# Expert weights of a 16-expert block moved in runs of 22,528 bytes per partition

## The chip, the cores and the metric

The kernel runs on one core of a Trainium2 chip. The metric is device time in microseconds (us) of one execution. The core has a matrix engine (PE, with PEld for its weight loads), a vector engine (DVE), a scalar engine (ACT), GpSimd (POOL) and a sync engine (SP) that here only issues DMAs; 16 DMA engines carry those transfers. SBUF has 128 partitions.

## The reference

One encoder block on 512 tokens of width 1,024, all in float32: a mixer (four pooling windows and eight heads of differential attention, merged by gates) and then a mixture of 16 experts, in which each expert picks its 64 tokens of highest affinity. The change is in the second half:

```python
    logits = jnp.einsum('bsd,de->bse', h, w_router, preferred_element_type=jnp.float32)
    aff = jax.nn.softmax(logits, axis=-1)
    vals, idx = lax.top_k(aff.transpose(0, 2, 1), cap)
    xs = jax.vmap(lambda hb, ib: hb[ib])(h, idx.reshape(B, -1)).reshape(B, N_EXPERTS, cap, D)
    g = jnp.einsum('becd,edf->becf', xs, w_gate)
    u = jnp.einsum('becd,edf->becf', xs, w_up)
    y = jnp.einsum('becf,efd->becd', jax.nn.silu(g) * u, w_down) * vals[..., None].astype(h.dtype)
    flat = (jnp.arange(B)[:, None, None] * S + idx).reshape(-1)
    out = jax.ops.segment_sum(y.reshape(-1, D), flat, num_segments=B * S)
```

Each expert has three matrices of 1,024 x 2,816 (or 2,816 x 1,024) float32 numbers, so 11,534,336 bytes each and 34.6 MB for the three. The result is added to the block's stream and goes through a last RMS norm.

## The kernel before

The first half (to about 480 us of the profiled execution) computes the mixer. Its weights come through four small tiles `wraw` of 2 KB per partition (L130, in `load_next`), are split into a high and a low part by ACT and POOL into three tiles `whl`, and feed three-pass matmuls. The last of these matrices is `w_out`, eight pieces `k` of two loads each; its loop `out_proj` runs until about 530 us and reads eight tiles `m0` to `m7`.

The second half walks through the experts `e`. The token matrix `xs` of 64 tokens is the stationary operand, the weights are the moving one, and two column groups of PE work at a time (L726 and L727 in `colpair`, one for each half of the output rows). For one expert, in order:

- gate and then up: eight slices `k` of 2,816 columns each (L737), a slice being one `slot`, 128 partitions of 11,264 bytes. A slice takes six matmuls in three pairs.
- SiLU, product, and eleven transposes into `hT2`.
- down: 22 row blocks `f` of 1,024 columns, two to a slot (L762). In SBUF a slot's partition gets two runs of 4,096 bytes.
- the sum into `acc` through `vv` (L774, L776), while the routing of the next expert is computed by DVE in between.

`slot()` deals out 13 buffers in a ring: NS1 = 7 of pool `s1`, then NS2 = 6 of pool `s2`. `s1` lies where the tiles of the first half were and is free when they are; `s2` lies over `m0` to `m7`, `whl` and `wraw` and is free as `out_proj` gets through them. All weights are requested by SP, in program order. Each request waits until the last matmul on the slot's former contents is done, and also until the transfer eight requests earlier has landed, since eight semaphores (DMAHW0 to DMAHW7) are dealt out in turn to SP's transfers.

For the last expert the down matrix is taken in two column halves `n` (L784), each in six slots of up to two row blocks of either half `h`, and a slot in two transfers with runs of 2,048 bytes (L795). After `n` = 0 its sum and squares are done (L805), `acc` is put into the result banks of `n` = 1 (L788), and after `n` = 1 the norm and the output follow (L810 to L821).

The Bass context is made with the standard scratch for descriptors of DMAs that GpSimd issues (L891); it takes 16,384 bytes of each partition. GpSimd issues 32 such DMAs, all in the mixer (L382, L388).

Of the kernel before, what the change touches and what calls it, by code (L numbers as in the profile page):

```python
# [9 lines left out]
F32 = mybir.dt.float32  # L10
# [7 lines left out]
P = 128  # L18
S = 512
D = 1024  # L20
KT = D // P
# [3 lines left out]
F = 2816  # L25
FH = F // 2
NF = F // P
NFH = NF // 2
NE = 16
CAP = 64  # L30
# [4 lines left out]
CHUNKS = ((0, 512), (512, 512), (1024, 384))  # L35
# [26 lines left out]
 'pool': (2, 2, 2, 1, 1, 0, 0, 0),  # L62
 'fills': (1, 0.3, 2, 0.5, 2.5, 1.5, 2, 1, 0.5),
 'tabs': 1}
NS1, NS2 = 7, 6


def block_kernel(tc, a, out):
    nc = tc.nc
    V, A, G, T, SP = nc.vector, nc.scalar, nc.gpsimd, nc.tensor, nc.sync  # L70
# [5 lines left out]
    def cols(i, n=P):  # L76
        return slice(i * n, (i + 1) * n)
# [135 lines left out]
    with pool("st", side="right") as st:  # L213
        first = []
# [34 lines left out]
        for k in range(KT):  # L249
            for j in range(2):  # L250
                w = loaded[j]
# [242 lines left out]
    for h in range(NH):  # L494
# [13 lines left out]
        o = at.tile([P, S], F32, name="o", bufs=2)  # L508
# [33 lines left out]
    for d in range(KT):  # L542
        w = weights()
        ps = bank("ip")
# [27 lines left out]
    s1 = ctx.enter_context(pool("s1"))  # L572
# [72 lines left out]
    for k in range(KT - 2):  # L645
        w = weights()
# [19 lines left out]
    s2 = ctx.enter_context(pool("s2", side="right"))  # L666
# [51 lines left out]
    def slot():  # L718
        i = nslot[0] % (NS1 + NS2)
        nslot[0] += 1  # L720
        if i < NS1:
            return s1.tile([P, F], F32, name="sl1", bufs=NS1)
        return s2.tile([P, F], F32, name="sl2", bufs=NS2)

    def colpair(ps, n, lhsT, r0, r1, first, last):
        T.matmul(ps[0:CAP, :n], lhsT, r0, start=first, stop=last)  # L726
        T.matmul(ps[CAP:, :n], lhsT, r1, start=first, stop=last)  # L727

    cur = route(0, rk0)
    for e in range(NE):  # L730
        xs, ga = cur
        proj = []
        for wname in ("w_gate", "w_up"):
            ps = [gu() for _ in CHUNKS]
            for k in range(KT):
                w = slot()
                SP.dma_start(w, a[wname][e, k])  # L737
                for i, (c0, n) in enumerate(CHUNKS):
                    colpair(ps[i], n, xs[:, k], w[:, c0:c0 + n], w[:, FH + c0:FH + c0 + n],
                            k == 0, k == KT - 1)  # L740
            proj.append(ps)
            if wname == "w_gate":
                rk = rank(e + 1) if e + 1 < NE else None
                vv = route_v(ga)
        cur = route(e + 1, rk) if e + 1 < NE else None
        act = act_tile()
        for i, (c0, n) in enumerate(CHUNKS):
            A.activation(act[:, c0:c0 + n], proj[0][i][:, :n], AF.Silu)
            V.tensor_tensor(act[:, c0:c0 + n], act[:, c0:c0 + n], proj[1][i][:, :n], op=ALU.mult)  # L749
        hT2 = tr_tile()  # L750
        for j0 in range(0, NFH, 4):
            n = min(4, NFH - j0)
            pt = mx()
            for j in range(n):
                T.transpose(pt[:, cols(j)], act[:, cols(j0 + j)], ident)  # L755
            A.copy(hT2[:, j0:j0 + n], pt[:, :n * P].rearrange("p (j q) -> p j q", j=n))  # L756
        if e == NE - 1:
            break
        pd = mx()
        for f0 in range(0, NF, 2):  # L760
            w = slot()
            SP.dma_start(w[:, :2 * D].rearrange("p (f c) -> p f c", f=2), a["w_down"][e, f0:f0 + 2].rearrange("f p c -> p f c"))  # L762
            for j in range(2):
                f = f0 + j
                half, ft = divmod(f, NFH)
                colpair(pd, S, hT2[:, ft, cols(half, CAP)],
                        w[:, j * D:j * D + S], w[:, j * D + S:(j + 1) * D], f == 0, f == NF - 1)
        y = mw.tile([P, S], F32, name="y", bufs=2)
        A.copy(y, pd)
        for t in range(NTT):  # L770
            for n in range(2):
                pc = mx()
                r = cols(n, CAP)
                T.matmul(pc, vv[r, cols(t)], y[r], start=True, stop=True)  # L774
                c = cols(n, S)
                V.tensor_tensor(acc[:, t, c], (x1 if e == 0 else acc)[:, t, c], pc, op=ALU.add)  # L776
# [7 lines left out]
    for n in range(2):  # L784
# [2 lines left out]
            for t in range(NTT):  # L787
                T.matmul(fin[t], ident, acc[:, t, c], start=True, stop=False)  # L788
        pd = mx()
        for j0 in range(0, NFH, 2):  # L790
            nj = min(2, NFH - j0)
            w = slot()[:, :2 * nj * S].rearrange("p (h j c) -> p h j c", h=2, j=nj)
            for h in range(2):
                f0 = h * NFH + j0
                SP.dma_start(w[:, h], a["w_down"][NE - 1, f0:f0 + nj, :, c].rearrange("f p c -> p f c"))  # L795
            for j in range(nj):
                for h in range(2):
                    T.matmul(pd[cols(h, CAP)], hT2[:, j0 + j, cols(h, CAP)], w[:, h, j],  # L798
                             start=(j0 + j == 0), stop=(j0 + j == NFH - 1))
# [45 lines left out]
    return {"consts": cv, "border": border, "tie": tie, "slots": slots}  # L845


def _layout(i):
    x = i["x"].reshape(S, D)
    w_in = i["w_in"].reshape(D, -1)  # L850
# [5 lines left out]
    def pk(v):  # L856
# [18 lines left out]
        "w_out": i["w_out"].reshape(KT, P, D),  # L875
        "g_ffn": pk(i["g_ffn"]),
        "w_router": i["w_router"].reshape(KT, P, NE).transpose(1, 0, 2),
        "w_gate": i["w_gate"].reshape(NE, KT, P, F),
        "w_up": i["w_up"].reshape(NE, KT, P, F),
        "w_down": i["w_down"].reshape(NE, NF, P, D),  # L880
        "g_final": i["g_final"].reshape(1, D),
    }

# [18 lines left out]
```

## Time and profile before

| | us |
|---|---|
| median of 3 runs (1854.99 to 1856.50) | 1855.67 |
| profiled execution, span from the first to the last instruction | 1854.6 |
| PE busy | 1692.7 (91%) |
| DVE busy | 565.4 (30%) |
| ACT busy | 333.1 (18%) |
| POOL busy | 228.9 (12%) |
| all 19,979 instructions; transfers on SP's queue | 602.04 MB, 114,976 packets |

The page cuts the span into 40 slices of 46.4 us and prints for each the busy tenths of every engine, the clock granted to PE, the busy tenths of the DMA engines and the bytes moved. A group of instructions is then shown with its line, engine and tiles. The chain of waits goes back from the last instruction to what released it, step by step. Windows give busy times and bytes moved for any stretch.

### The profile page before, as it was taken

What the parts mean: (1) busy time and instruction counts of PE and PEld (TensorE: products, weight loads), DVE (VectorE), ACT (ScalarE), POOL (GpSimd) and SP (SyncE); (2) the same over time, 40 slices, a digit from 0 to 9 for tenths busy, and PEclk for the clock granted to TensorE, in tenths of its full rate; (3) what the DMA queues carried; (4) which work ended last, traced back from release to release, by engine and by line L of the source; (5) the groups of instructions that cost most, each with busy time, mean ns of one, the idle gap of its engine ahead of it and who ended that gap; (6) DMA issues with size and microseconds to landing.
All of it is one profiled execution on the core that took longest, in us unless ns stands there. A gap on an engine that the chain in (4) does not pass through costs nothing.

```text
span 1854.6 us, 19979 instructions
## 1 busy us (share of the span) xinstructions
PE 1692.7 (91%) x7980; PEld 826.2 (45%) x7980; DVE 565.4 (30%) x1313; ACT 333.1 (18%) x647; POOL 228.9 (12%) x193
## 2 busy tenths in 40 slices
PE   7999999999989999999898989889898988889887
PEld 5777888778853333333232323223232323323222
DVE  6965566753150212202021211202121220202102
ACT  4454545563221000000000000000000000000001
POOL 2543444545500000000000000000000000000000
PEclk9999999999999999999999999999999999999999
DMA  5332222222789999999999999999999999999996
GB/s 197 97 97 86 82 89 80 69 78 82 267 331 413 421 418 417 421 414 425 414 423 415 420 418 417 422 414 424 415 422 417 418 421 415 423 415 423 415 409 260
DMA packets 117629, 607.52 MB, mean 328 GB/s; under 512 B 11936, under 2 KB 12576, under 8 KB 84768
## 3 DMA queue, kind: packets, MB, share of 16 engines
q1 hardware_dynamic: 114976, 602.04, 80.5%
q0 software_dynamic: 2560, 4.20, 1.1%
q8 instruction: 63, 1.03, 0.2%
q14 instruction: 30, 0.25, 0.0%
HBM read 599.90 MB, written 2.10 MB: 325 GB/s over the span
## 4 chain that ended last, share of the span: by engine, by line
PE 46%; DMA 43%; DVE 6%; issue 2%; ACT 1%; POOL 1%; SPq 0%; DVEq 0%; ACTq 0%; POOLq 0%
DMA sl<-in_w_up_dram 15%; DMA sl<-in_w_gate_dram 14%; DMA sl<-in_w_down_dram 14%; PE gu L726 12%; PE mx L726 6%; PE ip L98 5%; PE ip L100 5%; PE ip L99 5%; PE mx L774 2%; PE mx L692 2%; PE sc L98 1%; PE sc L100 1%; PE sc L99 1%; PE mx L798 1%; PE sc L441 1%
## 5 line engine op out<-in xcount | busy, mean ns | idle before, releaser
L726 PE MATMUL gu<-sl,xs 128*64 128x512 f32 (+1 forms) x1536 | 631.5, 562 | 24.5 <-DMA sl<-in_w_up_dram 24.1
L727 PE MATMUL gu<-sl,xs 128*64 128x512 f32 (+1 forms) x1536 | 631.8, 562 | 0.0
L726 PEld LDWEIGHTS gu<-sl,xs 128*64 128x64 f32 x1536 | 203.6, 137 | 412.9 <-issue 363.5
L726 PE MATMUL mx<-sl,hT 128*64 128x512 f32 x660 | 305.8, 600 | 55.4 <-DMA sl<-in_w_down_dram 50.4
L727 PE MATMUL mx<-sl,hT 128*64 128x512 f32 x660 | 306.1, 600 | 0.0
L726 PEld LDWEIGHTS mx<-sl,hT 128*64 128x64 f32 x660 | 81.5, 136 | 266.2 <-issue 139.5
L727 PEld LDWEIGHTS gu<-sl,xs 128*64 128x64 f32 x1536 | 200.1, 137 | 0.0
L93 POOL TENSOR_TENSOR whl<-wraw,whl 128x512 fp32r<-128x512 f32 x122 | 174.4, 1449 | 191.5 <-ACT whl L91 191.2
L776 DVE TENSOR_TENSOR acc<-acc,mx 128x512 f32<-128x512 f32 x112 | 72.5, 685 | 409.6 <-PE mx L774 409.6
L814 POOL TENSOR_TENSOR fs<-fs,cv 128x1 f32<-128x1 f32 x4 | 2.2, 554 | 1314.2 <-DVE fs L812 1314.2
L749 DVE TENSOR_TENSOR act<-act,gu 128x512 f32<-128x512 f32 (+1 forms) x48 | 30.5, 640 | 425.1 <-PE gu L727 425.1
L774 PE MATMUL mx<-y,vv 64*128 64x512 f32 x240 | 100.5, 684 | 27.7 <-DVE acc L776 16.5
L91 ACT ACTIVATE whl<-wraw 128x512 fp32r<-128x512 f32 (+1 forms) x149 | 86.8, 621 | 102.8 <-PE ip L100 44.2
L98 PE MATMUL ip<-hT,whl 128*128 128x512 f32 x240 | 98.4, 410 | 0.0
L99 PE MATMUL ip<-hT,whl 128*128 128x512 f32 x240 | 95.3, 397 | 0.0
L100 PE MATMUL ip<-hT,whl 128*128 128x512 f32 x240 | 94.8, 395 | 0.0
L692 PE MATMUL mx<-x,gm 128*64 128x512 f32 x256 | 74.4, 616 | 17.1 <-DVE gm L687 17.1
L694 ACT COPY y<-mx 128x512 f32<-128x512 f32 x16 | 9.4, 586 | 431.5 <-PE mx L692 431.5
L601 DVE TENSOR_SCALAR_CACHE_REDUCE cmp<-mx,aff 128x384 f32<-128x384 f32 (+3 forms) x105 | 54.7, 521 | 104.8 <-PE mx L672 102.7
L756 ACT COPY hT<-mx 128x512 f32<-128x512 f32 (+1 forms) x48 | 24.9, 552 | 323.8 <-PE mx L755 323.7
L727 PEld LDWEIGHTS mx<-sl,hT 128*64 128x64 f32 x660 | 81.5, 136 | 0.0
L774 PEld LDWEIGHTS mx<-y,vv 64*128 64x128 f32 x240 | 32.8, 193 | 93.9 <-DVE acc L776 69.6
(219 smaller groups left out, 1965.7 us busy)
## 6 DMA issues: line engine op xcount, KB each, us to landing
sl<-in_w_gate_dram SPq DMA_DIRECT2D x128, 1408.0 KB, 23.7
sl<-in_w_up_dram SPq DMA_DIRECT2D x128, 1408.0 KB, 27.1
sl<-in_w_down_dram SPq DMA_DIRECT2D x165, 1024.0 KB, 18.9
wraw<-in_w_c_dram SPq DMA_DIRECT2D x79, 256.0 KB, 2.9
sl<-in_w_down_dram SPq DMA_DIRECT2D x20, 512.0 KB, 10.7
wraw<-in_w_v_dram SPq DMA_DIRECT2D x16, 256.0 KB, 2.9
wraw<-in_w_pool_out_dram SPq DMA_DIRECT2D x16, 256.0 KB, 2.8
wraw<-in_w_attn_out_dram SPq DMA_DIRECT2D x16, 256.0 KB, 2.9
```

The lines of the kernel that those rows point to most:

```text
L91: A.activation(dst_h, src, AF.Copy, scale=scale)
L93: (eng or V).tensor_tensor(dst_l, src, dst_h.bitcast(F32), op=ALU.subtract)
L98: T.matmul(ps, lh, rh, start=first, stop=False)
L99: T.matmul(ps, lh, rl, start=False, stop=False)
L100: T.matmul(ps, ll, rh, start=False, stop=last)
L601: V.tensor_scalar(scratch(src.shape[-1]), src, thr, None, op0=op, op1=ALU.add, accum_out=dst)
L692: T.matmul(px[cols(n, CAP)], gm[:, t], x1[:, t, cols(n, S)], start=(t == 0), stop=(t == NTT - 1))
L726: T.matmul(ps[0:CAP, :n], lhsT, r0, start=first, stop=last)
L727: T.matmul(ps[CAP:, :n], lhsT, r1, start=first, stop=last)
L749: V.tensor_tensor(act[:, c0:c0 + n], act[:, c0:c0 + n], proj[1][i][:, :n], op=ALU.mult)
L774: T.matmul(pc, vv[r, cols(t)], y[r], start=True, stop=True)
L776: V.tensor_tensor(acc[:, t, c], (x1 if e == 0 else acc)[:, t, c], pc, op=ALU.add)
```

## The change

Gate and up are stored in DRAM so that two slices `k` of a partition lie side by side; a transfer fills one slot of 22,528 bytes per partition, and the loop over `k` becomes one over pairs `k2`. The down matrix of experts 0 to 14 is stored as four blocks per expert, each 22,528 bytes per partition: 5.5 row blocks. Row blocks 5 and 16 are cut between two slots, each side with 256 of the 512 columns of either column group, so that these two take four narrower matmuls where two stood. The last expert's down matrix becomes an array of its own, `w_last`, laid out by column half; each half comes in pieces of 4, 4 and 3 and of 4, 3, 2, 1 and 1 row-block pairs, a piece being one transfer with one run per partition. The ring has seven slots of double size, four in `s1` and three in `s2`. The scratch for GpSimd's descriptors is 2,048 bytes.

```diff
-NS1, NS2 = 7, 6
+NS1, NS2 = 4, 3
+F2 = 2 * F
+DOWN = 4
+LAST = (((0, 4), (4, 4), (8, 3)), ((0, 4), (4, 3), (7, 2), (9, 1), (10, 1)))
+def down_rows(b):
+    lo, hi = 11 * b, 11 * (b + 1)
+    out = []
+    while lo < hi:
+        if lo % 2 or hi - lo == 1:
+            out.append((lo // 2, lo % 2))
+            lo += 1
+        else:
+            out.append((lo // 2, None))
+            lo += 2
+    return out
...
-            return s1.tile([P, F], F32, name="sl1", bufs=NS1)
-        return s2.tile([P, F], F32, name="sl2", bufs=NS2)
+            return s1.tile([P, F2], F32, name="sl1", bufs=NS1)
+        return s2.tile([P, F2], F32, name="sl2", bufs=NS2)
...
-            for k in range(KT):
-                w = slot()
-                SP.dma_start(w, a[wname][e, k])
-                for i, (c0, n) in enumerate(CHUNKS):
-                    colpair(ps[i], n, xs[:, k], w[:, c0:c0 + n], w[:, FH + c0:FH + c0 + n],
-                            k == 0, k == KT - 1)
+            for k2 in range(KT // 2):
+                wd = slot()
+                SP.dma_start(wd, a[wname][e, k2])
+                for j in range(2):
+                    k, w = 2 * k2 + j, wd[:, j * F:(j + 1) * F]
+                    for i, (c0, n) in enumerate(CHUNKS):
+                        colpair(ps[i], n, xs[:, k], w[:, c0:c0 + n], w[:, FH + c0:FH + c0 + n],
+                                k == 0, k == KT - 1)
...
-        for f0 in range(0, NF, 2):
+        for b in range(DOWN):
             w = slot()
-            SP.dma_start(w[:, :2 * D].rearrange("p (f c) -> p f c", f=2), a["w_down"][e, f0:f0 + 2].rearrange("f p c -> p f c"))
-            for j in range(2):
-                f = f0 + j
+            SP.dma_start(w, a["w_down"][e, b])
+            o = 0
+            for f, q in down_rows(b):
                 half, ft = divmod(f, NFH)
-                colpair(pd, S, hT2[:, ft, cols(half, CAP)],
-                        w[:, j * D:j * D + S], w[:, j * D + S:(j + 1) * D], f == 0, f == NF - 1)
+                r = slice(0, S) if q is None else cols(q, 256)
+                n = r.stop - r.start
+                lhsT = hT2[:, ft, cols(half, CAP)]
+                first, last = f == 0, f == NF - 1
+                T.matmul(pd[0:CAP, r], lhsT, w[:, o:o + n], start=first, stop=last)
+                T.matmul(pd[CAP:, r], lhsT, w[:, o + n:o + 2 * n], start=first, stop=last)
+                o += 2 * n
...
-        for j0 in range(0, NFH, 2):
-            nj = min(2, NFH - j0)
-            w = slot()[:, :2 * nj * S].rearrange("p (h j c) -> p h j c", h=2, j=nj)
-            for h in range(2):
-                f0 = h * NFH + j0
-                SP.dma_start(w[:, h], a["w_down"][NE - 1, f0:f0 + nj, :, c].rearrange("f p c -> p f c"))
+        for j0, nj in LAST[n]:
+            w = slot()[:, :2 * nj * S]
+            SP.dma_start(w, a["w_last"][n, :, 2 * j0 * S:2 * (j0 + nj) * S])
+            w = w.rearrange("p (j h c) -> p h j c", h=2, j=nj)
...
-        "w_gate": i["w_gate"].reshape(NE, KT, P, F),
+        "w_gate": i["w_gate"].reshape(NE, KT // 2, 2, P, F).transpose(0, 1, 3, 2, 4).reshape(NE, KT // 2, P, F2),
...
-    nc = _bacc.Bacc("TRN2", target_bir_lowering=False, num_devices=1)
+    nc = _bacc.Bacc("TRN2", target_bir_lowering=False, num_devices=1, dynamic_dma_scratch_size=2048)
```

On SP's queue at the start of the experts, the first weights are requested between the last loads of `w_out`. `sl1` and `sl2` are slots of the two pools; the names in brackets are the semaphores waited for. Before:

```order
L737 DMA sl1_4770<-in_w_gate_dram 128x2816 [waits DMAHW7_49,DVE_49]
L130 DMA wraw_4447<-in_w_out_dram 128x512 [waits DMAHW0_49,Pool_49]
L130 DMA wraw_4451<-in_w_out_dram 128x512 [waits DMAHW4_49,DMAHW1_49,Pool_49]
L737 DMA sl1_4778<-in_w_gate_dram 128x2816 [waits DMAHW2_49,DMASW1_49,DMASW0_49]
L130 DMA wraw_4480<-in_w_out_dram 128x512 [waits DMAHW5_49,DMAHW3_49,Pool_49]
L130 DMA wraw_4484<-in_w_out_dram 128x512 [waits DMAHW6_49,Pool_49]
L737 DMA sl1_4786<-in_w_gate_dram 128x2816 [waits PE_49]
L737 DMA sl1_4794<-in_w_gate_dram 128x2816 [waits PE_49]
L737 DMA sl1_4802<-in_w_gate_dram 128x2816 [waits DMAHW7_49]
L737 DMA sl1_4810<-in_w_gate_dram 128x2816 [waits DMAHW0_49]
L737 DMA sl1_4818<-in_w_gate_dram 128x2816 [waits DMAHW1_49]
L737 DMA sl2_4826<-in_w_gate_dram 128x2816 [waits DMAHW2_49,DVE_49,PE_49]
```

The same place of SP's queue now:

```order
L756 DMA sl1_4770<-in_w_gate_dram 128x5632 [waits DMAHW7_49,DVE_49]
L149 DMA wraw_4447<-in_w_out_dram 128x512 [waits DMAHW0_49,Pool_49]
L149 DMA wraw_4451<-in_w_out_dram 128x512 [waits DMAHW4_49,DMAHW1_49,Pool_49]
L149 DMA wraw_4480<-in_w_out_dram 128x512 [waits DMAHW5_49,DMAHW2_49,Pool_49]
L149 DMA wraw_4484<-in_w_out_dram 128x512 [waits DMAHW6_49,DMAHW3_49,Pool_49]
L756 DMA sl1_4784<-in_w_gate_dram 128x5632
L756 DMA sl1_4798<-in_w_gate_dram 128x5632 [waits PE_49]
L756 DMA sl1_4812<-in_w_gate_dram 128x5632
L756 DMA sl2_4854<-in_w_up_dram 128x5632 [waits DMAHW7_49,DVE_49,PE_49]
L756 DMA sl2_4868<-in_w_up_dram 128x5632 [waits DMAHW1_49,DMAHW2_49,DMAHW0_49,DMAHW3_49,PE_49,Pool_49]
L756 DMA sl2_4882<-in_w_up_dram 128x5632 [waits PE_49]
L756 DMA sl1_4896<-in_w_up_dram 128x5632 [waits PE_49]
```

The first transfer of weights is twice as large and stands ahead of all four last loads of `w_out`; then four slots of `s1` hold all of the first gate matrix, `s2` takes the first three pairs of slices of up (the first of these waits for the matmuls on `m4`, before it was `m2` for a single slice), and the fourth waits for the first two slices of gate to be used up.

On SP's queue at the end, the first column half of the last expert's down matrix (and after the change both halves). Before:

```order
L795 DMA sl1_9563<-in_w_down_dram 128x2x512 [waits DMAHW2_49,PE_49]
L795 DMA sl1_9563<-in_w_down_dram 128x2x512 [waits DMAHW3_49]
L795 DMA sl1_9570<-in_w_down_dram 128x2x512 [waits DMAHW4_49,PE_49]
L795 DMA sl1_9570<-in_w_down_dram 128x2x512 [waits DMAHW5_49]
L795 DMA sl2_9577<-in_w_down_dram 128x2x512 [waits DMAHW6_49,PE_49]
L795 DMA sl2_9577<-in_w_down_dram 128x2x512 [waits DMAHW7_49]
L795 DMA sl2_9584<-in_w_down_dram 128x2x512 [waits DMAHW0_49,PE_49]
L795 DMA sl2_9584<-in_w_down_dram 128x2x512 [waits DMAHW1_49]
L795 DMA sl2_9591<-in_w_down_dram 128x2x512 [waits DMAHW2_49,PE_49]
L795 DMA sl2_9591<-in_w_down_dram 128x2x512 [waits DMAHW3_49]
L795 DMA sl2_9598<-in_w_down_dram 128x512 [waits DMAHW4_49,PE_49]
L795 DMA sl2_9598<-in_w_down_dram 128x512 [waits DMAHW5_49]
```

Now, with the three pieces of the first half and the five of the second:

```order
L818 DMA sl2_9157<-in_w_last_dram 128x4096 [waits DMAHW1_49,PE_49]
L818 DMA sl1_9167<-in_w_last_dram 128x4096 [waits DMAHW2_49,PE_49]
L818 DMA sl1_9177<-in_w_last_dram 128x3072 [waits DMAHW3_49,PE_49]
L818 DMA sl1_9212<-in_w_last_dram 128x4096 [waits DMAHW4_49,PE_49]
L818 DMA sl1_9222<-in_w_last_dram 128x3072 [waits DMAHW5_49,PE_49]
L818 DMA sl2_9230<-in_w_last_dram 128x2048 [waits DMAHW6_49,PE_49]
L818 DMA sl2_9236<-in_w_last_dram 128x1024 [waits DMAHW7_49,PE_49]
L818 DMA sl2_9240<-in_w_last_dram 128x1024 [waits DMAHW1_49,DMAHW0_49,PE_49]
```

Twelve transfers of the first half become three; the last of them holds three row-block pairs, where the last of before held one.

## Rows read from the trace of the kernel before

**Rows 1.** The page's 40 slices: PE and DMA busy tenths, bytes moved.

```profile
PE   7999999999989999999898989889898988889887
...
DMA  5332222222789999999999999999999999999996
GB/s 197 97 97 86 82 89 80 69 78 82 267 331 413 421 418 417 421 414 425 414 423 415 420 418 417 422 414 424 415 422 417 418 421 415 423 415 423 415 409 260
```

**Rows 2.** The chain that ended last, shares of the span by line.

```profile
DMA sl<-in_w_up_dram 15%; DMA sl<-in_w_gate_dram 14%; DMA sl<-in_w_down_dram 14%; PE gu L726 12%; PE mx L726 6%; PE ip L98 5%; PE ip L100 5%; PE ip L99 5%; PE mx L774 2%; PE mx L692 2%; PE sc L98 1%; PE sc L100 1%; PE sc L99 1%; PE mx L798 1%; PE sc L441 1%
```

**Rows 3.** The chain in order of time: start, us, what; a DMA from issue to landing.

```profile
611.06 1.18 PE mx L774 x4
...
685.46 1.18 PE mx L774 x4
...
1004.38 27.10 DMA sl<-in_w_gate_dram
1031.54 28.26 DMA sl<-in_w_up_dram
...
1069.12 18.82 DMA sl<-in_w_down_dram
...
1668.87 27.11 DMA sl<-in_w_gate_dram
```

**Rows 4.** Waits of SP's queue: waited for, us in total, times, longest.

```profile
SPq L737 <- DMA sl<-in_w_gate_dram: 330.3, 112, 3.4
SPq L762 <- PE gu L727: 196.8, 77, 6.2
```

**Rows 5.** The page's packets, by size.

```profile
DMA packets 117629, 607.52 MB, mean 328 GB/s; under 512 B 11936, under 2 KB 12576, under 8 KB 84768
```

**Rows 6.** Windows: stretch, its us, busy us by engine, clock, DMA share, GB/s.

```profile
1008.00:1056.00 48.00, 44.65 (x210) 16.43 (x208) 12.93 (x41) 2.27 (x4) 0.00 (x0) 1.00 1.01 423
1060.00:1084.00 24.00, 20.17 (x93) 6.40 (x93) 2.50 (x5) 1.55 (x3) 0.00 (x0) 1.00 1.02 409
...
1144.00:1168.00 24.00, 20.17 (x93) 6.29 (x89) 2.50 (x5) 1.55 (x3) 0.00 (x0) 1.00 1.03 412
...
1812.00:1832.00 20.00, 18.55 (x58) 6.34 (x54) 5.09 (x8) 3.48 (x9) 0.00 (x0) 1.00 1.04 385
```

**Rows 7.** SP's requests at the experts' start, in order of time.

```profile
510.68 0.33 SPq L737 DMA_DIRECT2D sl<-in_w_up_dram  x1
529.39 0.33 SPq L737 DMA_DIRECT2D sl<-in_w_up_dram  x1
530.07 1.36 SPq L737 DMA_DIRECT2D sl<-in_w_up_dram  x3
548.07 0.33 SPq L737 DMA_DIRECT2D sl<-in_w_up_dram  x1
550.43 0.33 SPq L737 DMA_DIRECT2D sl<-in_w_up_dram  x1
```

**Rows 8.** Windows at the experts' start.

```profile
500.00:520.00 20.00, 20.00 (x104) 16.56 (x103) 4.22 (x10) 4.85 (x11) 5.64 (x5) 1.00 1.00 408
...
524.00:532.00 8.00, 7.65 (x55) 6.51 (x54) 6.00 (x26) 4.17 (x10) 0.54 (x1) 1.00 0.41 141
...
544.00:548.00 4.00, 3.64 (x22) 1.90 (x24) 2.92 (x11) 0.23 (x1) 0.00 (x0) 1.00 0.14 59
```

**Rows 9.** PE's timeline after the last expert's weights land.

```profile
1821.50 2.79 PE L798 MATMUL mx<-sl,hT 128*64 128x512 f32 x10 [0.23 <-DMA sl<-in_w_down_dram]
1824.96 3.70 PE L805 MATMUL gu<-y,vv 128*128 128x512 f32 x8 [0.68 <-ACT y L801]
...
1832.03 9.66 PE L798 MATMUL mx<-sl,hT 128*64 128x512 f32 x44
```

**Rows 10.** The page's groups: the matmuls of down.

```profile
L726 PE MATMUL mx<-sl,hT 128*64 128x512 f32 x660 | 305.8, 600 | 55.4 <-DMA sl<-in_w_down_dram 50.4
```

**Rows 11.** The page's DMA issues of GpSimd: KB each, us to landing.

```profile
qx<-lt POOLq DMA_DIRECT2D x16, 128.0 KB, 2.5
```

More of the change, by code (lines that the diff above doesn't have):

```diff
@@ L845, in _shape_constants, with down_blocks @@
     return {"consts": cv, "border": border, "tie": tie, "slots": slots}
+def down_blocks(w):
+    w = w.reshape(-1, NF, P, 2, 2, 256)
+    rows = []
+    for b in range(DOWN):
+        for f, q in down_rows(b):
+            r = w[:, f] if q is None else w[:, f, :, :, q:q + 1]
+            rows.append(r.reshape(r.shape[0], P, -1))
+    return np.concatenate(rows, axis=2).reshape(-1, P, DOWN, F2).transpose(0, 2, 1, 3)
 def _layout(i):
@@ L877, in _layout @@
         "w_router": i["w_router"].reshape(KT, P, NE).transpose(1, 0, 2),
-        "w_gate": i["w_gate"].reshape(NE, KT, P, F),
-        "w_up": i["w_up"].reshape(NE, KT, P, F),
-        "w_down": i["w_down"].reshape(NE, NF, P, D),
+        "w_gate": i["w_gate"].reshape(NE, KT // 2, 2, P, F).transpose(0, 1, 3, 2, 4).reshape(NE, KT // 2, P, F2),
+        "w_up": i["w_up"].reshape(NE, KT // 2, 2, P, F).transpose(0, 1, 3, 2, 4).reshape(NE, KT // 2, P, F2),
+        "w_down": down_blocks(i["w_down"].reshape(NE, NF, P, D)[:NE - 1]),
+        "w_last": i["w_down"].reshape(NE, 2, NFH, P, 2, S)[NE - 1].transpose(3, 2, 1, 0, 4).reshape(2, P, NF * S),
         "g_final": i["g_final"].reshape(1, D),
```

## The prediction

> **What bounds the kernel now.** I read the 40 slices first. From the thirteenth slice on (about 560 us) the DMA engines are busy in every tenth and move 413 to 425 GB/s, while PE's digits fall back to 8 again and again [rows 1]: the transfers set the pace there, not PE. The chain of waits says the same: 43% of the span hangs on landings of up, gate and down weights [rows 2]. Its pieces in order of time show a repeating expert: a transfer of gate issued at 1004.38 lands after 27.10 us, one of up follows, then one of down, and eight experts later the same gate piece begins at 1668.87 [rows 3]. So one expert takes (1668.87 - 1004.38) / 8 = 83.06 us for 34.6 MB, 416.6 GB/s. What PE alone needs is read earlier, while slots were still full: from the sum of expert 0 to that of expert 1, 685.46 - 611.06 = 74.4 us [rows 3]. PE has 8.7 us to spare per expert. SP's own waits agree: it mostly waits for the landing eight requests back (112 times for gate, at most 3.4 us) and for PE to free a slot (at most 6.2 us) [rows 4], with the DMA engines busy meanwhile. The question is only what a byte costs in a longer run.
>
> **What a packet costs.** 117,629 packets less 84,768 under 8 KB leave 32,861 [rows 5]; gate and up have 256 x 128 = 32,768 partition runs, so a run of 11,264 bytes is one packet. A gate piece of the chain is eight transfers, since a request waits for the landing eight back: 1,024 packets, 64 on each of 16 engines, in 27.11 us, or 423.6 ns each (425.5 GB/s). Down, with runs of 4,096 bytes, shows as windows of 409 and 412 GB/s [rows 6]; at 410 a packet costs 4,096 x 16 / 410 = 159.8 ns and the matrix 28.13 us. The two give 263.8 ns for 7,168 bytes, 36.8 ps per byte, and 9.1 ns per packet. A third size tests the line: 2,048 bytes would cost 84.5 ns, 388 GB/s, and the last weights show 385 [rows 6]. For 22,528 bytes the line gives 9.1 + 829.0 = 838.1 ns, 430 GB/s, and a matrix (32 packets per engine) 26.82 us. Twice 27.11 plus 28.13 is 82.35 of the 83.06 us; 0.71 us I can't place, and I leave it as it is.
>
> The change goes beyond the longest run that the trace shows, so 838.1 is an extension of a line. Bounds: on one side 847.2 ns, two packets of 11,264 bytes; on the other, give down all of the 83.06 us that gate and up leave (28.84 us, 163.9 ns): 36.2 ps per byte, 15.5 ns per packet, 831.7 ns and 26.61 us. The 48 us window over gate and up has 423 GB/s, dips included [rows 6]; a line through 426.1 ns gives 844.6 ns and 27.03 us. I take 838.1, as the chain's pieces repeat to 0.01 us.
>
> The Trainium skill, "DMA: Bandwidth & Descriptors", Bandwidth, puts the ceiling of the DMA ports at 435.2 GB/s. By this estimate a matrix takes no less than 26.50 us, and the sum below could come to about -45 us at most; the trace so far agrees, as no slice stands above 425 GB/s [rows 1].
>
> **The change part by part.**
> - Down of experts 0 to 14 in longer runs: 15 x (28.13 - 26.82) = -19.7 us. All of it lies on the path, as transfers follow each other without a gap.
> - Gate and up: of 256 slices, 13 are requested before the first reuse of a slot and not paced by the stream; 243 / 8 = 30.4 matrices x (27.11 - 26.82) = -8.8 us.
> - Last expert: the first column half, 5.77 MB, at 385 GB/s takes 15.0 us; in runs of 16,384 and 12,288 bytes, by the line some 428 GB/s, 13.5 us: -1.5 us. The second half has time anyway: PE reaches it at 1832.03 [rows 9].
> - Fewer transfers, 12 instead of 27 per expert: 0. Eight transfers in a row take 3.39 us each, all inclusive, so what a single one costs is hidden by the others in flight.
> - The start. Before, nine slices are requested by 510.68, four more at 529.39 to 531, when `out_proj` is through, and then each 2.36 us one more, from 548.07 [rows 7]. The DMA engines run dry twice, at 524 to 532 (share 0.41) and 544 to 548 (0.14) [rows 8]. Now five double slots, ten slices, come before 529.39, four slices then, and the next request waits for two slices of gate: 550.43. So the stream restarts 2.36 us later with one slice (3.39 us) less to move: -1.0 us.
> - The end. After the landing at 1821.50 PE worked 2.79 us on the three last row-block pairs [rows 9], while the last 0.52 MB was still landing. Now these three pairs are one piece: it lands those 0.52 MB, 1.2 us, later, and then takes 3 x 9.66 / 11 = 2.6 us: +1.1 us. The rest of the tail stays.
> - The first big transfer now stands ahead of four loads of `w_out` instead of two: the first two of them come up to 3.4 us later. PE has no idle time at 500 to 520 [rows 8], working on buffers split earlier; a step of `out_proj` is over 5 us. Between 0 and +3.4, I take 0. If that cover is gone, all experts start that much later.
> - Four extra matmuls per expert in down: at 600 ns [rows 10] at most 2.4 us, 76.8 of PE against over 80 of the stream. 0.
> - A double slot comes free only after both halves. Seven hold 20.2 MB, 47 us of stream; the stream starves only if PE holds all of them, and SP's longest wait for PE in down is 6.2 us [rows 4]. 0.
> - Smaller scratch: 32 transfers of GpSimd, 2.5 us to landing [rows 11]. If each had to wait for the one before, and the path with it, 32 x 2.5 = 80 us; if the ring never fills, 0. They come in twos, 16 pairs in some 400 us, so I take 0.
>
> Sum: -19.7 - 8.8 - 1.5 - 1.0 + 1.1 = -29.9 us; 1854.6 - 29.9 = 1824.7 us of span. The median of before stands 1.07 us above the profiled span: **1825.8 us**. An expert would take 83.06 - 1.31 - 0.58 = 81.2 us.
>
> The skill's same page, Anatomy of one DMA, gives each transfer about 2.0 us on top of bytes over 436 GB/s; 15 fewer transfers would then save 30 us per expert. Its estimate for a slice is 5.3 us; the rows have 3.39 us [rows 3]. That price belongs to a transfer alone, not to a full queue, and stays out of the sum.
>
> **The rivals.**
> - *Long runs gain nothing more*: a run is cut into two packets of 11,264 bytes, so that it doesn't become what the diff says, or the rate is flat above 11 KB. Then down gains 15 x 1.02 = 15.3, gate and up 0, the last half 1.4: -15.3 - 1.4 - 1.0 + 1.1 = -16.6, 1839.1 us. For it: no longer run was seen. Against: three sizes lie on one line.
> - *A packet costs more than I think*: 831.7 ns above, with the 0.71 us belonging to down. Down 15 x 2.23 = 33.4, gate and up 30.4 x 0.50 = 15.2, the last half 1.6: -50.1, 1805.6 us. For it: it uses up the whole period. Against: the windows of down show 409 to 412, and this needs 400.
> - *Slower*: partition runs of 22,528 bytes put the 16 engines' streams twice as far apart in memory, and they get in each other's way. If that throws gate, up and down to the 410 GB/s of the 4 KB runs, gate and up lose 30.4 x 1.02 = 31.0, down stays, the last half gains 0.9: +30.2, 1885.9 us. It decides from (83.06 - 0.71) / 3 = 27.45 us a matrix, 420 GB/s: below that the kernel is slower. Against: doubling and more from 4,096 to 11,264 bytes only raised the rate; the margin is thin, though.
> - *No change*: the rate falls to 420 GB/s, or something at the start (`w_out`, GpSimd's ring) eats the gain.
>
> **How the numbers follow.** Forecast 0.53 (1818 to 1833; with the window's line 1830.6), flat 0.20, costlier packet 0.18, slower 0.06, no change 0.03. The predicted time is 1825.8 us. The range leaves out the slower and unchanged cases and half of the costlier packet, 0.18 together: 1807 to 1841. Faster by over 0.2% (about what a measurement of this kernel tells from no change) 0.91, within it 0.03, slower 0.06.
>
> **What would show it.** Packets of 8 KB and more falling to about 24,000, 47 x 4 x 128, with a few large ones besides, would show that a run is one packet (double that: cut). Four transfers in 26.8 us, the same for all three matrices, 430 GB/s in the windows with no dip at down, and a period near 81.2 us would show the line right; 27.1 us the flat rival; over 27.45 the slower one. The first reuse of a slot should be requested near 550, and the first half should be done some 30 us before the end. A DMA share below 1 between 560 and 1790 would make the slot argument wrong, a first matmul of gate later than before the one on `w_out`.

## The result, and the profile after

The changed kernel takes 1826.04 us (median of 4 runs, 1825.73 to 1827.96) where the kernel before takes 1855.94, timed beside it (4 runs): a ratio of 0.9838, 95% interval 0.9824 to 0.9852, 29.9 us less. The forecast was 1825.8 us. The profiled execution of after has a span of 1826.1 us; it is the slowest of its four runs (1827.96).

The page of after, with the lines that answer to [rows 1, 2, 5] (DMA busy tenths and bytes in 40 slices, here of 45.7 us; packets by size; shares of the chain by line):

```profile
DMA  6232322222598999999999999999999999999995
GB/s 200 90 101 81 93 81 81 70 70 90 201 387 378 430 428 430 429 428 429 429 429 426 432 427 431 427 431 428 429 430 428 429 429 429 429 430 428 429 426 235
DMA packets 58091, 607.49 MB, mean 333 GB/s; under 512 B 7952, under 2 KB 8592, under 8 KB 33168
DMA sl<-in_w_down_dram 22%; PE gu L745 20%; PE mx L791 7%; PE ip L117 5%; PE mx L800 5%; PE ip L119 5%; PE ip L118 5%; PE mx L711 3%; DVE cmp L620 3%; DMA sl<-in_w_last_dram 2%; DVE acc L802 2%; DVE cmp L623 1%; PE mx L822 1%; PE sc L460 1%; PE at L483 1%
```

From the fourteenth slice to the last but one the transfers move 426 to 432 GB/s; before, they swung between 409 and 425. 58,091 less 33,168 are 24,923 packets of 8 KB and more: 47 x 4 x 128 = 24,064 weight runs, 768 pieces of `w_last`, and some 90 others. So a run of 22,528 bytes is one packet. The chain, however, reads as if PE had become the bound: landings have 24% of it in the line above where they had 43%. It hasn't. SP's waits tell why (line, waited for: us in total, times, longest), the answer to [rows 4]:

```profile
SPq L756 <- PE gu L746: 405.3, 61, 20.1
...
SPq L756 <- PE mx L792: 309.9, 60, 11.6
...
SPq L756 <- DMA sl<-in_w_down_dram: 45.9, 38, 1.6
```

With seven buffers, the landing eight requests back is seldom what a request waits for; it mostly waits for PE to free the slot, up to 20.1 us. But the transfers never run out meanwhile, as two windows over the steady part show (stretch, its us, busy us by engine, PE's clock, DMA share, GB/s), which answer to [rows 6]:

```profile
1008.00:1056.00 48.00, 44.69 (x229) 17.10 (x227) 10.19 (x38) 3.76 (x7) 0.00 (x0) 1.00 1.00 428
...
1060.00:1084.00 24.00, 17.49 (x85) 5.90 (x82) 1.28 (x2) 0.59 (x1) 0.00 (x0) 1.00 0.99 425
```

The DMA share is 1.00 and 0.99, and PE is idle for 6.5 of the 24 us in the second. A long chain share of PE only says that PE's release was the last semaphore before a request that then stood in a queue that was full anyway. The dip of down to 409 is nearly gone (425).

For the period I take one event per expert that hangs on the stream: the matmul that waited for the last piece of down, for experts 4 and 14. In after (start, us, instruction, idle time before it):

```profile
913.00 0.43 PE L791 MATMUL mx<-sl,hT 128*64 128x256 f32 x1 [1.77 <-DMA sl<-in_w_down_dram]
...
1722.99 0.43 PE L791 MATMUL mx<-sl,hT 128*64 128x256 f32 x1 [1.74 <-DMA sl<-in_w_down_dram]
```

and in the kernel before:

```profile
921.88 0.64 PE L726 MATMUL mx<-sl,hT 128*64 128x512 f32 x1 [0.60 <-DMA sl<-in_w_down_dram]
...
1751.32 0.64 PE L726 MATMUL mx<-sl,hT 128*64 128x512 f32 x1 [0.60 <-DMA sl<-in_w_down_dram]
```

(1722.99 - 913.00) / 10 = 81.00 us per expert, where it was 82.94. The forecast said 81.2. Since these two events lie on the stream in both kernels, they also cut the two spans into pieces that can be compared:

| stretch | before | after | difference | forecast |
|---|---|---|---|---|
| start to the first gate request | 489.05 | 490.81 | +1.8 | 0 |
| from there to the last piece of down, expert 4 | 432.83 | 422.19 | -10.6 | -10.0 |
| ten experts | 829.44 | 809.99 | -19.5 | -18.9 |
| from there to the end | 103.28 | 103.11 | -0.2 | -1.0 |
| sum | 1854.6 | 1826.1 | -28.5 | -29.9 |

The forecast's column is its own sum, cut at the same places: five downs, 8.4 gate and up matrices and the start; ten of each three; two matrices, the last half and the tail. The first row is not part of the change: the first gate request comes at 488.1 to 490.8 us in the profiles of twelve kernels here, with no order by slots or runs; after's profile happens to stand at the late end.

### The profile page after: what moved, and what is told of

Read it like the earlier page. It is cut to its first block, busy times and chain, and to the rows that moved or that the text cites. A ratio compares the mean times of both kernels' runs of the same rounds, so it can differ in the third digit from the quotient of the medians.

```text
span 1826.1 us, 19721 instructions
## 1 busy us (share of the span) xinstructions
PE 1679.4 (92%) x8100; PEld 840.5 (46%) x8100; DVE 563.6 (31%) x1313; ACT 333.3 (18%) x647; POOL 227.5 (12%) x193
## 2 busy tenths in 40 slices
DMA packets 58091, 607.49 MB, mean 333 GB/s; under 512 B 7952, under 2 KB 8592, under 8 KB 33168
## 4 chain that ended last, share of the span: by engine, by line
PE 61%; DMA 25%; DVE 10%; issue 2%; ACT 2%; POOL 1%; SPq 0%; DVEq 0%; ACTq 0%; POOLq 0%
DMA sl<-in_w_down_dram 22%; PE gu L745 20%; PE mx L791 7%; PE ip L117 5%; PE mx L800 5%; PE ip L119 5%; PE ip L118 5%; PE mx L711 3%; DVE cmp L620 3%; DMA sl<-in_w_last_dram 2%; DVE acc L802 2%; DVE cmp L623 1%; PE mx L822 1%; PE sc L460 1%; PE at L483 1%
## 5 line engine op out<-in xcount | busy, mean ns | idle before, releaser
L745 PEld LDWEIGHTS gu<-sl,xs 128*64 128x64 f32 x1536 | 205.5, 138 | 400.6 <-issue 374.0
L791 PE MATMUL mx<-sl,hT 128*64 128x512 f32 (+1 forms) x720 | 293.2, 560 | 51.6 <-DMA sl<-in_w_down_dram 46.7
L792 PE MATMUL mx<-sl,hT 128*64 128x512 f32 (+1 forms) x720 | 293.2, 560 | 0.0
L746 PEld LDWEIGHTS gu<-sl,xs 128*64 128x64 f32 x1536 | 205.5, 138 | 0.0
L791 PEld LDWEIGHTS mx<-sl,hT 128*64 128x64 f32 x720 | 94.8, 137 | 236.1 <-issue 156.4
L792 PEld LDWEIGHTS mx<-sl,hT 128*64 128x64 f32 x720 | 94.8, 137 | 0.0
L711 PE MATMUL mx<-x,gm 128*64 128x512 f32 x256 | 60.7, 616 | 18.8 <-DVE gm L706 18.8
```

The source lines that it names most:

```text
L711: T.matmul(px[cols(n, CAP)], gm[:, t], x1[:, t, cols(n, S)], start=(t == 0), stop=(t == NTT - 1))
L791: T.matmul(pd[0:CAP, r], lhsT, w[:, o:o + n], start=first, stop=last)
L792: T.matmul(pd[CAP:, r], lhsT, w[:, o + n:o + 2 * n], start=first, stop=last)
```

## The experiments

The theory: a packet costs a fixed time and a time per byte on its engine, so that the length of the run in DRAM alone sets the gain. Its rivals: it is the number of transfers; it is the scratch or the larger ring; or the rate is flat above some length.

For the length of runs I measure periods, as above, from experts 4 to 14, here by ACT's copy of the expert's result (`y`), which every kernel has. In the kernel after it stands at

```profile
918.05 0.59 ACT L795 COPY y<-mx 128x512 f32<-128x512 f32 x1 [24.30 <-PE mx L792]
...
1728.04 0.59 ACT L795 COPY y<-mx 128x512 f32<-128x512 f32 x1 [24.34 <-PE mx L792]
```

again 81.00 us apart per expert.

**cut2 and cut8: after, with a slot's 22,528 bytes in two and in eight runs.** One transfer per slot as before; only DRAM is laid out so that a partition's bytes lie in R pieces. Same SBUF, same matmuls.

```diff
-                SP.dma_start(wd, a[wname][e, k2])
+                SP.dma_start(wd.rearrange("p (r c) -> p r c", r=RUNS), a[wname][e, k2].rearrange("r p c -> p r c"))
```

and the same for down; RUNS = 2 and 8.

> The changed kernel, with each slot still filled by one transfer, but the weights in DRAM laid out so that a partition gets two separate runs of 11,264 bytes. Packet theory (9.1 ns per packet and 36.8 ps per byte, and nothing else): a matrix takes 27.11 instead of 26.82 us, 45.3 matrices are paced by the stream, so 1826.0 + 13.1 = 1839 us, and windows near 425 GB/s. Transfer theory (what counts is that 12 transfers of 2.9 MB per expert replace 27 smaller ones): the transfers are the same, so 1826 us.

> As the one before, with eight runs of 2,816 bytes per partition and slot, still one transfer per slot. Packet theory: 9.1 + 103.6 = 112.7 ns per packet, 400 GB/s, 28.85 us a matrix, 1826.0 + 45.3 x 2.03 = 1918 us. Transfer theory: 1826 us.

Measured: cut2 1841.37 us (1839.52 to 1842.07), ratio to before 0.9917 (0.9902 to 0.9932); cut8 1930.37 us (1929.53 to 1930.94), 1.0398 (1.0382 to 1.0413). Packets and copies of `y` in cut2:

```profile
DMA packets 82155, 607.49 MB, mean 330 GB/s; under 512 B 7952, under 2 KB 8592, under 8 KB 33168
```

```profile
922.18 0.59 ACT L796 COPY y<-mx 128x512 f32<-128x512 f32 x1 [24.79 <-PE mx L793]
...
1741.55 0.59 ACT L796 COPY y<-mx 128x512 f32<-128x512 f32 x1 [24.66 <-PE mx L793]
```

and in cut8:

```profile
DMA packets 226540, 607.49 MB, mean 315 GB/s; under 512 B 7953, under 2 KB 8593, under 8 KB 225681
```

```profile
947.05 0.59 ACT L796 COPY y<-mx 128x512 f32<-128x512 f32 x1 [28.23 <-PE mx L793]
...
1828.54 0.59 ACT L796 COPY y<-mx 128x512 f32<-128x512 f32 x1 [28.37 <-PE mx L793]
```

The packets rise by 24,064 and by 168,449, as two and eight per partition run make; the periods are 81.94 and 88.15 us. With nothing but the runs changed, half of the gain over before is gone in cut2, and cut8 is slower than before. That the longer time was predicted to within 2.4 us for cut2 and fell short by 12 us for cut8 (1918 against 1930) says that the fixed cost of a packet is more than the 9.1 ns of the forecast.

**long45: after, with runs of 45,056 bytes.** Four slices to a slot, half of down to a slot, three slots; the last expert's column half comes into one slot, in the pieces of after.

```diff
-NS1, NS2 = 4, 3
-F2 = 2 * F
-DOWN = 4
+NS1, NS2 = 2, 1
+GRP = 4
+F2 = GRP * F
+DOWN = 2
```

> After with slots of 45,056 bytes per partition (four slices, or half of down), three of them, two and one; the last expert's column half sits in one such slot and comes in the same pieces. The line through the periods so far (37.0 ps per byte and about 10 ns per packet and engine) gives 1,677 ns for a run of 45,056 bytes and 80.5 us per expert where after has 81.0. At the start two slices fewer are loaded before the first reuse (6.8 us) and the reuse is requested two slices later (4.7 us): about 1826.0 - 0.5 x 13.5 + 11.5 = 1831 us. If the rate is flat above 22,528 bytes, 81.0 us per expert and 1838 us. If a run is cut into two packets of 22,528 bytes, 81.0 us too, with 24,000 packets instead of 12,000 over 8 KB. If three slots are too few, the DMA share falls below 1 in the steady part and the period rises above 81.

Measured: 1834.17 us (1833.62 to 1836.31), 0.9882 (0.9867 to 0.9897). Its packets, a window over the steady part, and the copies of `y`:

```profile
DMA packets 44552, 607.45 MB, mean 332 GB/s; under 512 B 6448, under 2 KB 7088, under 8 KB 31664
```

```profile
1008.00:1056.00 48.00, 43.34 (x204) 15.48 (x202) 12.84 (x41) 2.86 (x5) 0.00 (x0) 1.00 1.00 432
```

```profile
931.06 0.59 ACT L796 COPY y<-mx 128x512 f32<-128x512 f32 x1 [23.99 <-PE mx L793]
...
1734.66 0.59 ACT L796 COPY y<-mx 128x512 f32<-128x512 f32 x1 [18.88 <-PE mx L793]
```

12,888 packets of 8 KB and more, so a run of 45,056 bytes is one packet as well, and the period is 80.36 us (80.5 expected, 81.0 if flat). Four lengths now, from periods in which the stream is the bound. Each period is shared among the packets of one engine, so a figure also holds whatever else the period has in it:

| run, bytes | kernel | period, us | packets per engine | ns per packet |
|---|---|---|---|---|
| 2,816 | cut8 | 88.15 | 768 | 114.8 |
| 11,264 | cut2 | 81.94 | 192 | 426.8 |
| 22,528 | after | 81.00 | 96 | 843.8 |
| 45,056 | long45 | 80.36 | 48 | 1674.2 |

The line through the outer two is (1674.2 - 114.8) / 42,240 = 36.92 ps per byte and 10.8 ns per packet; it gives 426.7 and 842.5 for the inner two. So the line holds over a factor of 16, and there is no bend at 22,528. The fit is as good as the periods are: single experts scatter (long45's copies come 77.7 to 84.2 us apart), and from expert 5 instead of expert 4 on long45's period is 80.57 us, 0.3% more.

Why, then, is long45 slower than after? Its expert 4 is done 931.06 - 488.20 = 442.9 us after the first gate request, after's 918.05 - 490.81 = 427.2. Two windows at the start of long45:

```profile
520.00:528.00 8.00, 8.00 (x56) 7.04 (x56) 5.17 (x22) 2.98 (x9) 1.09 (x2) 1.00 0.00 0
...
544.00:552.00 8.00, 7.92 (x43) 2.90 (x43) 7.03 (x31) 0.00 (x0) 0.00 (x0) 1.00 0.10 38
```

With two slots in `s1` and a third only when `out_proj` is through, the stream stands still for all of 520 to 528, and nearly so for 544 to 552. At expert 4 it is 15.6 us behind after, which ten experts at 0.64 us less don't bring back. I had expected a loss of about 11.

**two_transfers: after, with two transfers of 11,264 bytes per partition for every slot.** This makes 24 transfers per expert (27 before, 12 in after), with the packets of cut2.

```diff
-                SP.dma_start(wd, a[wname][e, k2])
+                for s in range(2):
+                    SP.dma_start(wd[:, s * F:(s + 1) * F], a[wname][e, k2, :, s * F:(s + 1) * F])
```

> The changed kernel with its own layout in DRAM, but each slot filled by two transfers of half the columns: runs of 11,264 bytes again, 22,528 bytes apart, and 24 transfers per expert. Packet theory: 1839 us, the same as with one transfer of two runs. Transfer theory: 24 transfers are nearly the 27 of before, so most of the 29.9 us goes, about 1850 us. If runs that start 22,528 bytes apart get in each other's way, it is slower than the kernel with two runs in one transfer.

Measured: 1841.03 us (1840.75 to 1841.93), 0.9918 (0.9901 to 0.9935). cut2, with half the transfers and the same packets, has 1841.37. SP's queue is another one, though: it now waits for landings again.

```profile
SPq L757 <- DMA sl<-in_w_gate_dram: 338.1, 113, 4.1
...
SPq L757 <- DMA sl<-in_w_down_dram: 316.9, 105, 3.3
```

So neither the number of transfers nor what SP waits for moves the time; packets do. It is also the measurement that decides about the rule that the prediction left out: the Trainium skill, "DMA: Bandwidth & Descriptors", Anatomy of one DMA, puts a fixed cost of about 2.0 us on a transfer. That section is about transfers that GpSimd issues, which the prediction didn't say; these are SP's. Twelve more per expert would be 24 us per expert by it; in a queue that is never empty the two kernels differ by 0.3 us in all. So these runs don't show that cost in a full queue.

**down_11k: before, with down alone in runs of 11,264 bytes.** Eight single slots per expert instead of eleven transfers with runs of 4,096 bytes; gate, up, the last expert, ring and scratch as before.

```diff
-        for f0 in range(0, NF, 2):
+        for b in range(DOWN):
             w = slot()
-            SP.dma_start(w[:, :2 * D].rearrange("p (f c) -> p f c", f=2), a["w_down"][e, f0:f0 + 2].rearrange("f p c -> p f c"))
+            SP.dma_start(w, a["w_down"][e, b])
```

> The kernel before, with its 13 single slots and its gate and up; only down of experts 0 to 14 is laid out in eight slots of one run of 11,264 bytes (24 transfers per expert instead of 27). Packet theory: 15 x (28.13 - 27.11) = 15.3 us less than before, 1855.9 - 15.3 = 1840.6 us, and down's windows rise from 410 to 425 GB/s. Transfer theory: 3 of the 15 transfers saved, a fifth of 29.9 us, 1850 us.

Measured: 1841.80 us (1840.65 to 1842.91), 0.9921 (0.9906 to 0.9936), 14.6 us below before. A window over gate and up, and two over down at the places of [rows 6]:

```profile
1008.00:1056.00 48.00, 46.84 (x214) 17.31 (x214) 10.43 (x37) 2.27 (x4) 0.00 (x0) 0.93 1.01 424
1060.00:1084.00 24.00, 21.31 (x123) 8.33 (x122) 0.16 (x1) 1.69 (x4) 0.00 (x0) 1.00 1.01 423
1144.00:1168.00 24.00, 18.05 (x94) 6.32 (x92) 1.46 (x3) 0.58 (x1) 0.00 (x0) 1.00 1.01 422
```

409 and 412 have become 423 and 422. So half of the gain is down's way from 4,096 to 11,264 bytes, and the other half is everybody's way from 11,264 to 22,528 (cut2 to after, 15.3 us; the two were not timed side by side, and the kernel before was 0.4 us slower beside cut2).

**scratch, ring14, slots4: the covers that the prediction put at nothing.** Before with the small scratch alone; before with the small scratch and 8 + 6 single slots (the bytes of after's ring); after with four double slots, three and one, instead of seven.

```diff
-    nc = _bacc.Bacc("TRN2", target_bir_lowering=False, num_devices=1)
+    nc = _bacc.Bacc("TRN2", target_bir_lowering=False, num_devices=1, dynamic_dma_scratch_size=2048)
```

> The kernel before with nothing changed but the scratch for GpSimd's descriptors, 2,048 instead of 16,384 bytes. Theory: nothing waits for the ring, 1855.9 us, and the first gate transfer is requested at 489 us as before. Rival (the small ring holds GpSimd up in the mixer): later than 489 us, by the 1.8 us that the changed kernel shows there or more, and 1858 us or more.

```diff
-NS1, NS2 = 7, 6
+NS1, NS2 = 8, 6
```

> The kernel before with 14 single slots (eight and six) instead of 13, in the memory that the smaller scratch frees: the capacity of the changed kernel without its runs. Packet theory: one slice more is loaded before the stream is paced, 3.4 us, so 1852.5 us, and the windows stay at 425 and 410 GB/s. Rival (the gain came from the larger ring): most of the 29.9 us, under 1840 us.

```diff
-NS1, NS2 = 4, 3
+NS1, NS2 = 3, 1
```

> The changed kernel with four double slots (three and one) instead of seven. Theory that slots matter at the start alone: 8 instead of 14 slices are loaded by the time the first slot is used again, six slices of 3.35 us, 1826 + 20 = 1846 us, with the DMA share at 1 from about 570 us on and 430 GB/s. Rival (a double slot, free only when both halves are used, starves the stream once there are few): a DMA share clearly below 1 in every expert, a period above 83 us instead of 81.0, over 1855 us.

Measured: scratch 1856.91 us (11 runs, 1855.62 to 1857.76), ratio 1.0004 (0.9995 to 1.0012), first gate request at 488.8; ring14 1854.23 us (11 runs, 1852.37 to 1855.47), 0.9986 (0.9977 to 0.9995); slots4 1845.89 us (1845.03 to 1846.87), 0.9942 (0.9929 to 0.9956). The small scratch costs nothing by itself, and what it pays for, one slice more in the ring, brings 2 us (3.4 expected), not 29. slots4 loses 20 us to after, but all by expert 4, whose copy of `y` comes 447.7 us after the first gate request (427.2 in after). Two of its windows, one of the start and one of the steady part:

```profile
540.00:552.00 12.00, 11.23 (x52) 3.98 (x50) 6.59 (x29) 0.58 (x1) 0.00 (x0) 0.88 0.08 21
...
1008.00:1056.00 48.00, 43.56 (x182) 15.54 (x180) 13.10 (x41) 2.85 (x5) 0.00 (x0) 0.89 1.00 427
```

The stream waits from 540 to 552 (share 0.08), since six slices fewer are in SBUF; later the share is 1.00, the period 81.02 us. So four double slots are enough for the steady part, and the other three are worth their 20 us only as a stock for the start.

**fin_early and fin_pieces: what the tail leaves.** After, with the matmuls that put `acc` into the result banks (L814) moved ahead of both column halves, where PE waits for weights; and the same with the first half in pieces of 4, 2, 2, 2 and 1 row-block pairs.

```diff
+    for t in range(NTT):
+        T.matmul(fin[t], ident, acc[:, t, cols(1, S)], start=True, stop=False)
     for n in range(2):
         c = cols(n, S)
-        if n == 1:
-            for t in range(NTT):
-                T.matmul(fin[t], ident, acc[:, t, c], start=True, stop=False)
```

```diff
-LAST = (((0, 4), (4, 4), (8, 3)), ((0, 4), (4, 3), (7, 2), (9, 1), (10, 1)))
+LAST = (((0, 4), (4, 2), (6, 2), (8, 2), (10, 1)), ((0, 4), (4, 3), (7, 2), (9, 1), (10, 1)))
```

> After with the four pairs of matmuls that put acc into the result banks moved from between the last two column halves to before them, where PE waits for weights. The stream theory: PE's 3.6 us leave the tail behind the last landing that PE waits for, 1826.0 - 3.6 = 1822.4 us, and the first half ends where it did. Rival: they hold up the last matmuls of up by as much, and the time stays 1826; or the second half's weights then land too late for PE, and only 1 to 2 us are gained.

> The same, and the first column half in pieces of 4, 2, 2, 2 and 1 row-block pairs instead of 4, 4 and 3. The last piece then takes PE 0.9 us after its landing instead of 2.6, but PE, at 0.88 us a pair against 1.22 of the stream, has still to catch up with the pieces before it: 1.5 us earlier by that count, 1826.0 - 3.6 - 1.5 = 1820.9 us. If the tail of the last piece doesn't count, 1822.4.

Measured: fin_early 1822.73 us (1821.94 to 1824.04), ratio to before 0.9819 (0.9803 to 0.9835); fin_pieces 1823.12 us (1822.69 to 1823.23), 0.9820 (0.9805 to 0.9835). PE's tail in after, which answers to [rows 9]:

```profile
1782.71 1.09 PE L776 MATMUL mx<-ident,act 128*128 128x128 f32 x8
...
1789.15 6.58 PE L822 MATMUL mx<-sl,hT 128*64 128x512 f32 x28 [0.92 <-DMA sl<-in_w_last_dram]
1796.41 3.70 PE L829 MATMUL gu<-y,vv 128*128 128x512 f32 x8 [0.68 <-ACT y L825]
1799.95 3.60 PE L814 MATMUL gu<-acc,ident 128*128 128x512 f32 x8
1803.47 9.66 PE L822 MATMUL mx<-sl,hT 128*64 128x512 f32 x44
1813.88 3.70 PE L834 MATMUL gu<-y,vv 128*128 128x512 f32 x8 [0.74 <-ACT y L825]
```

in fin_early:

```profile
1781.12 1.09 PE L776 MATMUL mx<-ident,act 128*128 128x128 f32 x8
...
1787.31 6.58 PE L821 MATMUL mx<-sl,hT 128*64 128x512 f32 x28 [0.32 <-DMA sl<-in_w_last_dram]
1794.56 3.89 PE L828 MATMUL gu<-y,vv 128*128 128x512 f32 x8 [0.67 <-ACT y L824]
1798.38 9.66 PE L821 MATMUL mx<-sl,hT 128*64 128x512 f32 x44
1808.79 3.70 PE L833 MATMUL gu<-y,vv 128*128 128x512 f32 x8 [0.74 <-ACT y L824]
```

and the first half in fin_pieces:

```profile
1782.57 1.09 PE L776 MATMUL mx<-ident,act 128*128 128x128 f32 x8
...
1784.78 9.66 PE L821 MATMUL mx<-sl,hT 128*64 128x512 f32 x44
1795.12 3.89 PE L828 MATMUL gu<-y,vv 128*128 128x512 f32 x8 [0.69 <-ACT y L824]
```

From the sum of the first half to that of the second it is 17.47 us in after and 14.23 in fin_early: the 3.24 us are gone, and the first half is no later, counted from the transposes (13.70 and 13.44 us). The time follows, 3.3 us below after's median; the two were not timed side by side, but their runs don't overlap. It is the fastest kernel of this study, 34.1 us below the kernel before that was timed beside it. The smaller pieces bring nothing that the times can tell (1.5 us expected). In the trace they do shorten the first half, to 12.55 us, and PE's 44 matmuls then run without a gap, so PE, not the last landing, is the bound there. These 0.9 us are still there at the end: from the transposes to the end of the span it is 1821.0 - 1781.12 = 39.9 us in fin_early and 1821.5 - 1782.57 = 38.9 in fin_pieces. The profile of fin_pieces had fallen 1.5 us behind before its transposes, in a part that the change doesn't touch; whether the same hides the gain in the medians isn't shown.

## Why the prediction was right, step by step

- **The bound.** The step that carried everything, that the transfers set the pace from 560 us on and that a byte's price is a matter of runs, held: cut2 and cut8 change nothing else and move the time by 15.3 and 104.3 us.
- **The price of a packet.** Forecast 9.1 ns and 36.8 ps per byte, 838.1 ns for 22,528 bytes. The 843.8 of the table is not the same thing, since it shares out the whole period. A packet alone shows where PE waits for one landing after the other. In after:

```profile
980.31 0.43 PE L791 MATMUL mx<-sl,hT 128*64 128x256 f32 x1 [1.25 <-DMA sl<-in_w_down_dram]
987.01 0.64 PE L791 MATMUL mx<-sl,hT 128*64 128x512 f32 x1 [1.76 <-DMA sl<-in_w_down_dram]
993.73 0.43 PE L791 MATMUL mx<-sl,hT 128*64 128x256 f32 x1 [1.77 <-DMA sl<-in_w_down_dram]
```

  and in cut2:

```profile
1074.70 0.64 PE L792 MATMUL mx<-sl,hT 128*64 128x512 f32 x1 [1.84 <-DMA sl<-in_w_down_dram]
1081.49 0.43 PE L792 MATMUL mx<-sl,hT 128*64 128x256 f32 x1 [1.84 <-DMA sl<-in_w_down_dram]
```

  A transfer of eight packets per engine takes 6.71 us in after, 838.8 ns a packet, and of sixteen 6.79 us in cut2, 424.4 ns (forecast 423.6): 36.8 ps per byte and 10 ns. So the price was right to 0.1%; its fixed part, 10 ns, was put a little low. Twelve transfers at 6.71 us are 80.5 of the 81.00 us, and about 0.5 us per expert is something else, as the 0.71 us were that the forecast couldn't place and left as they were. Much of those can be placed: the forecast took 27.11 us for gate and for up, but its own piece of up at 1031.54 has 28.26 [rows 3]. In the chain of before an undisturbed piece of up takes as long as one of gate,

```profile
949.08 27.13 DMA sl<-in_w_up_dram
```

  but the nine that start from there to 1696.05 take 26.74 to 28.26 us and 27.56 in the mean, 0.45 more than 27.11. What holds the longer ones up is not shown. The "near" line through 426.1 ns, set aside, would have had 844.6 ns and 1830.6 us, too much in both. Had the price gone wrong by more, the time would have been off by the error times 32 packets times 45 matrices.
- **Down, -19.7.** By shares of the period, cut2's gives 27.31 us for a matrix in runs of 11,264 bytes; 82.94 - 2 x 27.31 leaves 28.32 for down before (the forecast had 28.13), and 15 x (28.32 - 27.00) = 19.8. It is also a fifth point for the line: 28.32 us for 176 packets are 160.9 ns for 4,096 bytes, where 10.8 ns and 36.92 ps per byte would give 162.0. The part of it up to 11,264 bytes was measured alone in down_11k: 14.6 us, where the flat rival's term said 15.3.
- **Gate and up, -8.8.** 30.4 x (27.31 - 27.00) = 9.4.
- **The start, -1.0.** SP's requests in after, the answer to [rows 7]:

```profile
490.81 0.33 SPq L756 DMA_DIRECT2D sl<-in_w_gate_dram  x1
...
506.54 45.66 SPq L756 DMA_DIRECT2D sl<-in_w_up_dram  x4
```

  The last of these four is the first reuse, at 506.54 + 45.66 less its own 0.33, 551.9, which is 61.1 us behind the first gate request; before, 548.07 - 489.05 = 59.0. It was to come 2.36 us later and came 2.0 later. The windows agree with the slice more that is loaded meanwhile (answer to [rows 8]; the third is new, the wait for two slices):

```profile
524.00:532.00 8.00, 7.81 (x49) 6.47 (x49) 5.77 (x22) 2.91 (x9) 0.54 (x1) 1.00 0.86 338
...
544.00:548.00 4.00, 3.23 (x20) 1.48 (x18) 1.55 (x5) 0.59 (x1) 0.00 (x0) 1.00 0.43 186
...
548.00:552.00 4.00, 4.00 (x22) 1.44 (x20) 3.75 (x19) 0.00 (x0) 0.00 (x0) 1.00 0.00 0
```

  Up to expert 4 the forecast's terms make -10.0, and -10.6 was measured.
- **`w_out` behind a larger transfer, 0.** Expert 0's sum comes 612.51 - 490.81 = 121.7 us after the first gate request in after, and 611.06 - 489.05 = 122.0 before [rows 3, 7]. The cover held.
- **Last expert and tail, -1.5, -0.6 and +1.1.** Together -1.0; measured -0.2, the one stretch that fell short. After's last eleven row-block pairs show where the mechanism was too coarse. The forecast let the half end 2.6 us of work after the last landing. But behind the second piece's landing at 1789.15 PE goes through 28 matmuls in 6.58 us without waiting again; it is still at work on the second piece when the third lands, and the half ends 6.58 us after the second landing. The first half is done 1826.1 - 1795.7 = 30.4 us before the end, as forecast.
- **Slots, scratch, extra matmuls, fewer transfers, 0 each.** slots4, scratch and two_transfers measured three of these alone; in the steady part, at its place or in the whole, each is 0. The extra matmuls of down were not taken out by themselves; PE has idle time there (6.5 of 24 us in the window above).
- **Too much and too little.** In the profiles the errors are -0.6 (to expert 4), -0.6 (ten experts), +0.8 (the end) and +1.8 for the mixer, which the change doesn't touch; against the medians the sum is off by 0.2 us. That this is smaller than any of its parts is luck.
- **The rivals.** *Flat*, or a run cut in two: 1839.1 forecast; cut2, which makes just that, has 1841.4, and after's packet count rules it out. *Costlier packet*, 15.5 ns: needs 831.7 ns, and 838.8 was measured for the packet alone, 843.8 with all of the period. *Slower* by streams in each other's way: 428 GB/s at 22,528 bytes and 432 at 45,056 in the windows, no sign of it.

## What to carry to other kernels

When a stream of weights is the bound and its queue is never empty, count packets, not transfers: in these runs each run per partition cost its engine 10 to 11 ns on top of 37 ps per byte, so runs of 4 KB lose about 5% against runs of 22 KB, and doubling beyond that gains less than 1%. Pay for longer runs with fewer, larger slots only as far as the stock at the start allows; what four double slots or three quadruple ones lost, they lost at the start and not in the steady part. And read the DMA share beside the chain: a chain that moves from landings to PE doesn't mean that the bound has moved.

## What the runs showed that I had not expected

- The line doesn't bend: 114.8, 426.8, 843.8 and 1674.2 ns for runs of 2,816 to 45,056 bytes lie on one straight line to within 0.2% (4,096 bytes lie 0.7% under it). Its slope is 16 / 36.92 ps = 433 GB/s, an estimate for endless runs. The ceiling of 435.2 GB/s in the Trainium skill, "DMA: Bandwidth & Descriptors", Bandwidth, fits: 430.6 GB/s over ten experts of long45 is the highest long mean here.
- The bound stayed and the chain changed its face: landings 43% before, 24% after, with the DMA share at 1.00 in both.
- One transfer or two for the same packets: 1841.4 and 1841.0 us.
